# Every fourth unit of weights gets its low part from an accumulating DMA

## The chip, the cores and the metric

The kernel runs on one core of one Trainium2 chip. The metric is the device time of one execution in microseconds. The kernel before takes 2758.89 us, the median of 2 runs (2758.85 to 2758.94).

A core has a matrix engine (TensorE, PE in the profile), a vector engine (VectorE, DVE), a scalar engine (ScalarE, ACT), GpSimd (POOL) and a sync engine (SyncE, SP), each with its own queue of instructions, worked off in order. Transfers are issued from a queue (here almost all from SyncE's) and carried out by 16 DMA engines.

## The reference

A decoder trunk of two layers for 256 tokens of width 2048, all in float32: first a retention layer, then a layer of block-sparse attention; each is followed by a squared-ReLU MLP and a gated embedding of the layer. Cut to its products with weights:

```
h = x
h = h + retention(rms_norm(h, ret_norm_g), ret_w_in, ret_w_out)      # w_in 2048 x 12288, w_out 4096 x 2048
h = h + square(relu(rms_norm(h, mlp_norm_g[0]) @ mlp_w_up[0])) @ mlp_w_down[0]   # 2048 x 8192, 8192 x 2048
h = h + (p[0] @ ple_w_up[0]) * sigmoid(rms_norm(h, ple_norm_g[0]) @ ple_w_gate[0])
k, v = split(rms_norm(h, kv_norm_g) @ w_kv)                          # 2048 x 4096
h = h + attention(rms_norm(h, att_norm_g) @ att_w_q, k, v, rel_bias) @ att_w_o
h = h + mlp(h, layer 1);  h = h + gated embedding(h, layer 1)
return rms_norm(h, final_norm_g)
```

With 256 tokens nearly all of the work is these products, and each weight is read from HBM once.

## The kernel before

**Units.** All weights are cut on the host into units of 128 x 1024 numbers (`UC = 1024`), 968 in all, in the order in which they are used: retention's inputs 0 to 191, its output 192 to 255, the up and down projections of the first MLP 256 to 511, embedding and gate to 547, attention to 675, the second MLP 676 to 931, and embedding and gate to 967. Two units make one transfer of 1024 KB into a tile `raw` of three buffers, issued by SyncE in `load`.

**High and low.** A product in float32 is made of three faster ones in a type of fewer bits (`F32R`): with w = wh + wl and x = xh + xl it is wh xh + wl xh + wh xl. So every unit is converted in `conv`: ScalarE copies `raw` to `wh`, which rounds it (L221), and VectorE subtracts, wl = raw - wh (L222). Both lines are in the helper `split`, which activations use as well. `wh` and `wl` have a ring of `LOOK + 1` = 4 buffers each.

**The loop.** `run` goes over the units in order. For unit i it puts the load of unit i + 6 on SyncE's queue, the conversion of unit i + `LOOK` (3) on ScalarE's and VectorE's, the matmuls of unit i on TensorE's, and then the tasks that were entered for i: emptying PSUM, normalisation, transposes, parts of the attention. There is no scheduler; the order of this code is the order on each queue. Since the ring has four buffers, the conversion of unit i + 3 waits for the matmuls of unit i - 1.

**The matmuls of a unit.** In the up projection and for queries and keys (`phase_a`, `mm_a`, lines L153 and L155) weights are the stationary operand: 8 matmuls of 512 columns with wh and 8 of 256 with wl. Two units make one output tile; the first of them takes high before low, the second (`turned`) low before high. Elsewhere (`phase_b`, `mm_b`, lines L195 to L197) the activations are stationary: 12 matmuls of 512 columns, in threes of which the second reads wl. Products collect in four PSUM banks; `fold` (L226, L227) or the evacuation of the phase empties them.

**The end.** The last project (`last`) keeps its last four units, `hold = LOOK + 1`, until all are there, and then works them off for one half of the tokens and the other, so that the first half's final norm runs beside the second half's matmuls.

Of the kernel before, what the change touches and what calls it, by code (L numbers as in the profile page):

```python
# [10 lines left out]
F32 = mybir.dt.float32  # L11
F32R = mybir.dt.float32r
I32 = mybir.dt.int32
AF = mybir.ActivationFunctionType
ALU = mybir.AluOpType
# [5 lines left out]
KD = D // P  # L21
# [10 lines left out]
NEG = -1e30  # L32
UC = 1024
LEAD = 4
LOOK = 3
WARM = 9
FILL = 5
BR = 32
# [32 lines left out]
class Core:  # L71
# [24 lines left out]
    def conv(self, i):  # L96
        if i >= len(self.units):
            return
        raw = self.raws.pop(i)[:, self.units[i][1] % 2, :]
        wh = self.wp.tile([P, UC], F32R, name=f"wh{i}", tag="wh", bufs=LOOK + 1)  # L100
        wl = self.wp.tile([P, UC], F32R, name=f"wl{i}", tag="wl", bufs=LOOK + 1)
        self.split(wh, wl, raw)
        self.ready[i] = (wh, wl)

    def run(self):
        for fn in self.tasks.pop(-1, []):
            fn()
        for i in range(2, LOOK):
            self.conv(i)
        for i in range(len(self.units)):  # L110
            self.load(i + 6)
            self.conv(i + LOOK)
            wh, wl = self.ready.pop(i)
            self.units[i][2](wh, wl)
            for fn in self.tasks.pop(i, []):
                fn()
        while self.tasks:
            for fn in self.tasks.pop(min(self.tasks)):
                fn()
# [25 lines left out]
    def mm_a(self, ps, wh, wl, rhs, first, last, turned=False):  # L145

        mm = self.nc.tensor.matmul
        cut = [slice(k * P, (k + 1) * P) for k in range(8)]
        for low in (True, False) if turned else (False, True):
            for k, c in enumerate(cut):  # L150
                end = last and k == 7 and low != turned
                if low:
                    mm(ps[:, S:], wl[:, c], rhs[k][:, :S], start=False, stop=end)  # L153
                else:
                    mm(ps, wh[:, c], rhs[k], start=first and k == 0, stop=end)  # L155
# [35 lines left out]
    def mm_b(self, ps, wh, wl, x, t, j, first, last):  # L191

        mm = self.nc.tensor.matmul
        c, a, b = slice(j * 512, (j + 1) * 512), slice(t * P, (t + 1) * P), slice(S + t * P, S + (t + 1) * P)
        mm(ps, x[:, a], wh[:, c], start=first, stop=False)  # L195
        mm(ps, x[:, a], wl[:, c], start=False, stop=False)  # L196
        mm(ps, x[:, b], wh[:, c], start=False, stop=last)  # L197
# [101 lines left out]
    def start(self):  # L299
# [35 lines left out]
        self.xx = {}  # L335
        wh = self.wp.tile([P, UC], F32R, name="wh0", tag="wh", bufs=LOOK + 1)
        wl = self.wp.tile([P, UC], F32R, name="wl0", tag="wl", bufs=LOOK + 1)
        for n in range(2):
# [259 lines left out]
    def last(self, st, src):  # L598


        nc = self.nc
        per, hold = KD // 2, LOOK + 1
        b = len(self.units)
        fin = {"ssq": {}}

        def gains():
            for c in range(4):
                fin["g", c] = self.slot(f"gf{c}")
                row = self.io["gfin"]
                nc.sync.dma_start(fin["g", c], bass.AP(tensor=row.tensor, offset=row.offset + c * 512, ap=[[0, P], [1, 512]]))  # L610
        self.at(b, gains)

        def flip():
            for c in range(4):
                nc.vector.tensor_scalar_mul(fin["g", c], fin["g", c], -1.0 / 8192.0)
        self.at(b + 4, flip)

        def gate(c, t, bank, cuts=1):
            s = self.slot("gt")
            h = self.h[c][:, t]  # L620
            parts = [slice(i * 512 // cuts, (i + 1) * 512 // cuts) for i in range(cuts)]
            if c == 0:
                fin["ssq"][t] = self.cp.tile([P, 4 + t], F32, name=f"fssq{t}")
            for p in parts:
                nc.scalar.activation(s[:, p], bank[:, p], AF.Sigmoid, scale=fin["rn"][:, t:t + 1])
            if cuts > 1:
                scale(0, 1)
            for i, p in enumerate(parts):
                nc.vector.tensor_mul(s[:, p], s[:, p], st["up"][c, t][:, p])
                nc.vector.tensor_add(h[:, p], h[:, p], s[:, p])  # L630
                nc.scalar.activation(self.slot("sq")[:, p], h[:, p], AF.Square, accum_out=fin["ssq"][t][:, c + i:c + i + 1])
            if cuts == 1:
                nc.vector.tensor_mul(h, h, fin["g", c])

        def evac(c, banks, i):
            if c == 0:
                fin["rn"] = self.rn
            for t in range(2):
                gate(c, t, banks[t])
        for c in range(3):  # L640
            self.phase_b(f"gl{c}_", src, c * per, per, lambda k: st["x"][k], lambda banks, c=c: evac(c, banks, 0))
        banks, held = [], []

        def mm(wh, wl, u):
            if u == 0:
                banks.extend(self.bank(f"gl3_{t}_") for t in range(2))
            held.append((u, wh, wl))
            if per - hold <= u < per - 1:
                return
            for t in range(2):  # L650
                for v, h, l in held:
                    for j in range(2):
                        self.mm_b(banks[t], h, l, st["x"][2 * v + j], t, j, v + j == 0, v == per - 1 and j == 1)
                if u == per - 1:
                    if t:
                        gate(3, 1, banks[1], 2)
                        for c in (0, 2, 3):
                            scale(0, c)
                        norm(1)
                        for c in (0, 1, 3, 2):  # L660
                            scale(1, c)
                    else:
                        gate(3, 0, banks[0])
                        norm(0)
            held.clear()

        def norm(t):
            m = self.cp.tile([P, 1], F32, name=f"fm{t}")
            nc.vector.reduce_sum(m, fin["ssq"][t], axis=AX.X)
            fin["r", t] = self.rsqrt(None, m, RMS_EPS, 1, 1.0 / D)  # L670

        def scale(t, c):
            r = fin["r", t]
            h = self.h[c][:, t]
            if (t, c) == (1, 3):
                nc.vector.scalar_tensor_tensor(h, h, r, fin["g", c], op0=ALU.mult, op1=ALU.mult)
            elif c == 0:
                nc.vector.tensor_scalar_mul(h, h, r)
            else:
                nc.scalar.activation(h, h, AF.Copy, scale=r)  # L680
            q = nc.scalar if (t, c) == (1, 2) else nc.sync
            q.dma_start(self.io["out"][t * P:(t + 1) * P, c * 512:(c + 1) * 512], h)
        for u in range(per):
            self.unit(src, 3 * per + u, lambda wh, wl, u=u: mm(wh, wl, u))
# [216 lines left out]
```

## Time and profile before

| | |
|---|---|
| median of the runs shown | 2758.89 us |
| span of the profiled execution, first to last instruction | 2756.9 us |
| TensorE busy | 2743.4 us, 13744 matmuls |
| VectorE busy | 1694.6 us |
| ScalarE busy | 1322.8 us |
| GpSimd busy | 0.2 us |
| conversions of a whole unit, high (L221) | 966, 1051 ns each |
| conversions of a whole unit, low (L222) | 966, 1225 ns each |
| moved by DMA | 522.48 MB, 190 GB/s |

The profiled execution's own time is its span; how it stands to the median is told where the sum is made. A row of a group reads: line, engine, operation, output and inputs with their shapes, count, then busy us and mean ns of one, then the idle time ahead of it and what ended that. A row of the timeline begins with its start and its length in us. A row of waits gives who waited for whom, the sum in us, how often, and the longest. PEld is TensorE's loading of stationary operands, which overlaps with its matmuls.

### The profile page before, as it was taken

To read this page: it belongs to the slowest core of one execution; us is meant where nothing else is said; L and a number is where in the kernel's file an instruction comes from. 1 tells how busy PE (TensorE), PEld (TensorE's weight loads), DVE (VectorE), ACT (ScalarE), POOL (GpSimd) and SP (SyncE) were. 2 spreads that over 40 slices of the span, in tenths; PEclk is the share of its full clock that TensorE was granted. 3 is DMA by queue.
4 is the path that set the end of the run, shared out by engine and by line. 5 is a ranking of instruction groups with operands and counts; after the bars stand their busy time and mean duration, and the time that the engine had idled before them with its cause. 6 is when DMAs were issued, how large, how long until landed. Compare 5 with 4: busy or idle time off the path is not lost.

```text
span 2756.9 us, 34160 instructions
## 1 busy us (share of the span) xinstructions
PE 2743.4 (100%) x13744; PEld 2334.7 (85%) x13744; DVE 1694.6 (61%) x2321; ACT 1322.8 (48%) x1844; POOL 0.2 (0%) x4
## 2 busy tenths in 40 slices
PE   9999999999999999999999999999999999999998
PEld 7888888888888888888888888888888888888886
DVE  6766666655576544665546777775666446664555
ACT  6444444444454433454445555554544334544454
POOL 0000000000000000000000000000000000000000
PEclk9999999999999999999999999999999999999999
DMA  7455555555555555555565555555555555555554
GB/s 277 177 186 186 186 186 186 186 183 186 185 195 186 196 194 190 192 188 192 186 204 188 185 182 179 182 178 185 187 190 192 195 188 196 185 193 189 186 199 153
DMA packets 79450, 522.48 MB, mean 190 GB/s; under 512 B 8987, under 2 KB 12988, under 8 KB 17596
## 3 DMA queue, kind: packets, MB, share of 16 engines
q1 hardware_dynamic: 78476, 519.20, 53.1%
q10 hardware_dynamic: 816, 1.11, 0.3%
q8 instruction: 107, 1.75, 0.3%
q14 instruction: 51, 0.42, 0.0%
HBM read 517.39 MB, written 2.88 MB: 189 GB/s over the span
## 4 chain that ended last, share of the span: by engine, by line
PE 98%; DMA 1%; DVE 0%; ACT 0%; issue 0%; SPq 0%; ACTq 0%; DVEq 0%
PE up L155 17%; PE up L153 9%; PE qk L155 4%; PE aq L155 2%; PE ak L155 2%; PE qk L153 2%; PE aq L153 1%; PE ak L153 1%; PE pu L573 1%; DMA raw<-ret_in 1%; PE xt L255 1%; PE y L461 1%; PE dn__11046 L195 0%; PE dn__20748 L196 0%; PE dn__21353 L197 0%; PE dn__11358 L196 0%
## 5 line engine op out<-in xcount | busy, mean ns | idle before, releaser
L222 DVE TENSOR_TENSOR wl<-raw,wh 128x1024 fp32r<-128x1024 f32 (+1 forms) x971 | 1180.0, 1221 | 652.7 <-ACT wh L221 639.2
L221 ACT CAST wh<-raw 128x1024 fp32r<-128x1024 f32 (+1 forms) x971 | 1013.5, 1048 | 709.3 <-DVE rs_y L278 29.2
L155 PE MATMUL up<-x,wh 128*128 128x512 f32 x2048 | 490.5, 391 | 0.0
L155 PEld LDWEIGHTS up<-x,wh 128*128 128x128 f32 x2048 | 376.1, 188 | 72.4
L153 PEld LDWEIGHTS up<-x,wl 128*128 128x128 f32 x2048 | 263.4, 191 | 10.4
L153 PE MATMUL up<-x,wl 128*128 128x256 f32 x2048 | 266.7, 283 | 0.0
L226 ACT COPY t<-up 128x256 f32<-128x256 f32 x128 | 47.6, 372 | 331.6 <-PE up L155 331.6
L227 DVE TENSOR_TENSOR t<-t,up 128x256 f32<-128x256 f32 x128 | 53.9, 421 | 216.7 <-ACT t L226 216.5
L155 PE MATMUL qk<-x,wh 128*128 128x512 f32 x448 | 109.9, 393 | 0.0
L155 PEld LDWEIGHTS qk<-x,wh 128*128 128x128 f32 x448 | 81.8, 188 | 15.5
L233 ACT ACTIVATE x<-xt,g 128x256 fp32r<-128x256 f32 x112 | 52.5, 478 | 50.6 <-DVE x L234 39.4
L234 DVE SCALAR_TENSOR_TENSOR x<-xt,g,x 128x256 fp32r<-128x256 f32 x112 | 53.0, 481 | 25.7 <-ACT x L233 25.5
L155 PE MATMUL aq<-x,wh 128*128 128x512 f32 x256 | 63.3, 392 | 0.0
L155 PE MATMUL ak<-x,wh 128*128 128x512 f32 x256 | 62.9, 392 | 0.0
L153 PEld LDWEIGHTS qk<-x,wl 128*128 128x128 f32 x448 | 57.4, 191 | 2.2
L153 PE MATMUL qk<-x,wl 128*128 128x256 f32 x448 | 58.1, 283 | 0.0
L533 DVE SCALAR_TENSOR_TENSOR s<-t 128x256 f32<-128x256 f32 x128 | 54.4, 425 | 4.4
L155 PEld LDWEIGHTS ak<-x,wh 128*128 128x128 f32 x256 | 46.7, 189 | 8.7
L155 PEld LDWEIGHTS aq<-x,wh 128*128 128x128 f32 x256 | 46.5, 189 | 8.7
L222 DVE TENSOR_TENSOR a<-s,a 128x256 fp32r<-128x256 f32 x128 | 53.6, 419 | 0.0
L221 ACT CAST a<-s 128x256 fp32r<-128x256 f32 x128 | 52.0, 406 | 0.0
L242 ACT ACTIVATE sq<-h 128x512 f32<-128x512 f32 x48 | 30.1, 628 | 37.5 <-DVE h L542 15.6
(895 smaller groups left out, 4999.3 us busy)
## 6 DMA issues: line engine op xcount, KB each, us to landing
raw<-mlp_up SPq DMA_DIRECT2D x128, 1024.0 KB, 4.8
raw<-mlp_dn SPq DMA_DIRECT2D x128, 1024.0 KB, 4.8
raw<-ret_in SPq DMA_DIRECT2D x94, 1024.0 KB, 4.8
raw<-att SPq DMA_DIRECT2D x48, 1024.0 KB, 4.8
raw<-ret_out SPq DMA_DIRECT2D x32, 1024.0 KB, 4.8
raw<-ple_gate SPq DMA_DIRECT2D x32, 1024.0 KB, 4.8
raw<-att_o SPq DMA_DIRECT2D x16, 1024.0 KB, 4.8
raw<-ple_up SPq DMA_DIRECT2D x4, 1024.0 KB, 4.8
```

The source lines that it names most:

```text
L153: mm(ps[:, S:], wl[:, c], rhs[k][:, :S], start=False, stop=end)
L155: mm(ps, wh[:, c], rhs[k], start=first and k == 0, stop=end)
L221: self.nc.scalar.copy(dst_h, src)
L222: self.nc.vector.tensor_sub(dst_l, src, dst_h.bitcast(F32))
L226: self.nc.scalar.copy(dst, ps[:, :S])
L227: self.nc.vector.tensor_add(dst, dst, ps[:, S:])
L233: self.nc.scalar.activation(t[:, :S], src, AF.Copy, scale=gs)
L234: self.nc.vector.scalar_tensor_tensor(t[:, S:], src, gs, t[:, :S].bitcast(F32), op0=ALU.mult, op1=ALU.subtract)
L242: self.nc.scalar.activation(self.slot("sq"), self.h[c][:, t], AF.Square, accum_out=self.ssq[:, t, c:c + 1])
L255: self.nc.tensor.transpose(ps[:, o * P:(o + 1) * P], self.h[c][:, t, f * P:(f + 1) * P], self.ident)
L461: mm(ys[t], a, w, start=i == 0, stop=i == len(ops) - 1)
L533: nc.vector.scalar_tensor_tensor(s, t, 0.0, t, op0=ALU.max, op1=ALU.mult)
```

## The change

For units from 12 on whose index is 1 modulo 4, VectorE no longer makes the low part. ScalarE copies `raw` to `wh` as before and then writes -wh into `wl`, a copy with scale -1. Then GpSimd issues a DMA that reads the same 512 KB of weights from HBM a second time and adds them to what is in `wl`: raw - wh again. The ring of `wh` and `wl` grows from four to five buffers (`LOOK = 4`), and the conversion of a unit is put on the queues four units ahead rather than three, from the twelfth unit on; up to there it stays at three (`SOON`). The number of units held in the last project is now a constant (`HOLD = 4`), the same as before. The space in SBUF that is kept for the descriptors of software-issued transfers is set to 1024 bytes of a partition.

```diff
-LOOK = 3
+LOOK = 4
+SOON = 3
+HOLD = 4
+EVERY = 4
...
         wh = self.wp.tile([P, UC], F32R, name=f"wh{i}", tag="wh", bufs=LOOK + 1)
         wl = self.wp.tile([P, UC], F32R, name=f"wl{i}", tag="wl", bufs=LOOK + 1)
-        self.split(wh, wl, raw)
+        if i >= 12 and i % EVERY == 1:
+            src, j, _ = self.units[i]
+            self.nc.scalar.copy(wh, raw)
+            self.nc.scalar.activation(wl, wh.bitcast(F32), AF.Copy, scale=-1.0)
+            self.nc.gpsimd.dma_start(wl, self.io[src][j // 2, :, j % 2], accum_op=ALU.add)
+        else:
+            self.split(wh, wl, raw)
         self.ready[i] = (wh, wl)
...
-        for i in range(2, LOOK):
-            self.conv(i)
+        done = 2
         for i in range(len(self.units)):
             self.load(i + 6)
-            self.conv(i + LOOK)
+            while done <= i + (SOON if i < 12 else LOOK):
+                self.conv(done)
+                done += 1
...
-        per, hold = KD // 2, LOOK + 1
+        per, hold = KD // 2, HOLD
...
-    nc = bacc.Bacc("TRN2", target_bir_lowering=False, num_devices=1)
+    nc = bacc.Bacc("TRN2", target_bir_lowering=False, num_devices=1, dynamic_dma_scratch_size=1024)
```

Lines below the edit move by up to ten: L221, L222 and L226 of before are L231, L232 and L236 after; the two new ScalarE lines are L107 and L108, the DMA is L109. How it stands on the queues is shown at two places. The number behind a name is that of the unit or tile and, behind a second underscore, of the buffer; in brackets stand the semaphores that the instruction waits for (DMASW is one of a software-issued transfer, DMAHW one of SyncE's).

On ScalarE's queue, in the second half of the first up projection, before:

```order
L221 CAST wh408_9358<-raw408_9282 128x1024 [waits DMAHW7_49,PE_49,Activation_49]
L226 COPY t_9378<-up1_10_9339 128x256 [waits PE_49]
L221 CAST wh409_9386<-raw408_9282 128x1024 [waits Activation_49]
L221 CAST a10_9383<-s2_9381 128x256 [waits DVE_49]
L221 CAST wh410_9409<-raw410_9333 128x1024 [waits DMAHW0_49,PE_49,Activation_49]
```

The same place after:

```order
L231 CAST wh408_9438<-raw408_9385 128x1024 [waits DMAHW7_49]
L231 CAST a9_9435<-s2_9433 128x256 [waits DVE_49]
L107 CAST wh409_9461<-raw408_9385 128x1024 [waits PE_49]
L108 ACTIVATE wl409_9462<-wh409_9461 128x1024 [waits DMASW6_49,PE_49,Activation_49]
L236 COPY t_9482<-up1_10_9442 128x256 [waits PE_49]
L231 CAST wh410_9490<-raw410_9436 128x1024 [waits DMAHW0_49]
```

Unit 409 is converted one unit earlier, ahead of the copy that empties tile 10, and that copy now stands behind the negation.

On TensorE's queue, where unit 337 begins in the first down projection, before:

```order
L195 MATMUL dn0_1_0__8003<-wh337_7963,a2_6260 128x512 [waits Activation_49]
L196 MATMUL dn0_1_0__8003<-wl337_7964,a2_6260 128x512 [waits DVE_49]
L197 MATMUL dn0_1_0__8003<-wh337_7963,a2_6260 128x512
L195 MATMUL dn0_1_1__8004<-wh337_7963,a2_6260 128x512
L196 MATMUL dn0_1_1__8004<-wl337_7964,a2_6260 128x512
```

The same after:

```order
L205 MATMUL dn0_1_0__8089<-wh337_8030,a2_6328 128x512 [waits Activation_49]
L206 MATMUL dn0_1_0__8089<-wl337_8031,a2_6328 128x512 [waits DMASW1_49]
L207 MATMUL dn0_1_0__8089<-wh337_8030,a2_6328 128x512
L205 MATMUL dn0_1_1__8090<-wh337_8030,a2_6328 128x512
L206 MATMUL dn0_1_1__8090<-wl337_8031,a2_6328 128x512
```

The matmuls are the same and in the same order; the first that reads the low part waits for a transfer in place of VectorE.

## The prediction

> **What bounds the kernel now.** I read the shares of busy time first, then the waits of TensorE, then one stretch of the timeline, and last the transfers.
>
> ```profile
> span 2756.9 us, 34160 instructions
> PE 2743.4 (100%) x13744; PEld 2334.7 (85%) x13744; DVE 1694.6 (61%) x2321; ACT 1322.8 (48%) x1844; POOL 0.2 (0%) x4
> PEclk9999999999999999999999999999999999999999
> PE 98%; DMA 1%; DVE 0%; ACT 0%; issue 0%; SPq 0%; ACTq 0%; DVEq 0%
> PE warm L364 <- DVE zero L357: 1.5, 1, 1.5
> PE qk L182 <- ACT wh L221: 0.8, 2, 0.4
> ```
>
> The first four lines are of the page, the last two are all that the view of waits has for TensorE. A busy TensorE need not be at its peak, since the ends of matmuls are modelled; the waits say it better. In 2756.9 us TensorE waits 1.5 + 0.8 = 2.3 us for another engine, all of it in the first microseconds. The clock is granted nearly in full. So the end is set by the number of matmuls times their spacing, and no other engine has a share in it as long as it delivers on time.
>
> Is the spacing itself stretched by what VectorE, ScalarE or the transfers do beside it? Two windows of 8 us answer that, the first near the end, where the weights have all arrived, the second in a down projection. The columns are PE, PEld, DVE, ACT and POOL busy time with counts, the granted clock, the DMA share and GB/s.
>
> ```profile
> 2737.00:2745.00 8.00, 8.00 (x37) 6.64 (x36) 3.16 (x9) 1.41 (x3) 0.00 (x0) 1.00 0.00 0
> 1001.00:1009.00 8.00, 8.00 (x37) 6.62 (x36) 3.68 (x3) 3.16 (x3) 0.00 (x0) 1.00 0.49 184
> ...
> 2737.15 0.39 PE L196 MATMUL gl__22264<-wl,x 128*128 128x512 f32 x1
> ...
> 2740.33 0.39 PE L195 MATMUL gl__22265<-wh,x 128*128 128x512 f32 x1
> ```
>
> Both hold 37 matmuls, one with no transfer at all and one at 184 GB/s. Between the two starts shown lie 14 spacings: (2740.33 - 2737.15)/14 = 0.227 us. A unit of a projection is 12 such matmuls, 12 x 0.227 = 2.72 us, and that is what the rhythm of the down projection gives too, by its conversions:
>
> ```profile
> 1003.72 1.05 ACT L221 CAST wh<-raw 128x1024 fp32r<-128x1024 f32 x1 [1.67 <-PE dn__8004 L197]
> 1006.44 1.05 ACT L221 CAST wh<-raw 128x1024 fp32r<-128x1024 f32 x1 [1.67 <-PE dn__8004 L197]
> ...
> 1108.01 3.82 PE L155 MATMUL up<-x,wh 128*128 128x512 f32 x16
> 1113.58 3.82 PE L155 MATMUL up<-x,wh 128*128 128x512 f32 x16
> ```
>
> ScalarE converts one unit each 2.72 us and idles 1.67 us before it, for TensorE to give back a buffer. In the up projection two units take 1113.58 - 1108.01 = 5.57 us, 2.78 us each.
>
> **What is removed, and its worth.** Of 968 units, those with index 13, 17, ..., 965 change: 239. Each loses one VectorE subtraction and gains one ScalarE pass.
>
> ```profile
> L222 DVE TENSOR_TENSOR wl<-raw,wh 128x1024 fp32r<-128x1024 f32 x966 | 1177.2, 1225 | 651.1 <-ACT wh L221 637.7 <-PE aq L155 1.0
> L221 ACT CAST wh<-raw 128x1024 fp32r<-128x1024 f32 x966 | 1011.2, 1051 | 707.6 <-DVE rs_y L278 29.2 <-PE dn__18284 L197 26.7 <-PE dn__18008 L197 26.7
> L221 ACT CAST wh<-raw 128x512 fp32r<-128x512 f32 x3 | 1.7, 615 | 0.0
> L680 ACT ACTIVATE h<-h,rs_y 128x512 f32<-128x512 f32 x5 | 3.4, 712 | 1.3 <-DVE rs_y L278 1.3
> ```
>
> VectorE loses 239 x 1.225 = 293 us, from 1694.6 to 1402 us, 51% of the span. Nobody waits for it: TensorE's list of waits has no subtraction in it. So this is worth 0 us.
>
> ScalarE gains 239 scaled copies of 128x1024. A copy without scale costs 1.051 us; at 512 columns a scaled one costs 712 ns against 615, so the bound above is 1.051 + 2 x 0.097 = 1.25 us. I take 1.1: 263 us, from 1322.8 to 1586, 58%. Its cover is the 1.67 us of idle ahead of each conversion; were that gone, the pass would delay the next conversion by 1.1 us, and that has most of four units to spare. What stands behind the pass on ScalarE's queue are the copies that empty PSUM (L226); a bank is asked for again three tiles, some 16 us, later in the up projection. 0 us.
>
> **The wait that is added.** The first matmul on such a low part waited for VectorE and now waits for the transfer, and everything on TensorE's queue stands behind it. So the question of the case is a latency against a window. A unit's buffers come free when the unit five earlier is done, and it is due four units later. The rows of one unit's start, in the down projection (first two) and in the up projection:
>
> ```profile
> 1003.52 0.39 PE L195 MATMUL dn__8003<-wh,a 128*128 128x512 f32 x1
> 1003.74 0.39 PE L196 MATMUL dn__8003<-wl,a 128*128 128x512 f32 x1
> ...
> 1111.66 2.08 PE L153 MATMUL up<-x,wl 128*128 128x256 f32 x16
> ...
> 1111.91 1.05 ACT L221 CAST wh<-raw 128x1024 fp32r<-128x1024 f32 x1
> ```
>
> Down: the cast starts at 1003.72, as shown above, and the low part that it begins is read by the second matmul of the unit four later, 1003.74 + 4 x 2.72 = 1014.62. That is 10.9 us, less the cast, 1.05, the negation, 1.1, and some 0.1 for two hand-overs: 8.7 us are left for GpSimd's issue and the transfer. Up: of the sixteen low matmuls eight end one unit and eight begin the next, so the unit changes at about 1112.7; the cast, which needs only the high buffer, is done at 1112.96, the negation some 1.2 us later, 1114.2, and the low part is due at 1112.7 + 4 x 2.78 = 1123.8: 9.6 us.
>
> What it takes is not in the trace: no row shows GpSimd issuing a transfer, and none an accumulating one. The nearest:
>
> ```profile
> raw<-mlp_up SPq DMA_DIRECT2D x128, 1024.0 KB, 4.8
> h<-xn SPq DMA_DIRECT2D x4, 512.0 KB, 10.6
> out<-h SPq DMA_DIRECT2D x7, 256.0 KB, 2.4
> 17.70 0.56 SPq L370 DMA_DIRECT2D h<-xn  x1
> q1 hardware_dynamic: 78476, 519.20, 53.1%
> ```
>
> Below: a line through 256 KB in 2.4 us and 1024 KB in 4.8 puts a plain 512 KB at 3.2 us, and SyncE's issue at 0.56: 3.8 us. Above: the 512 KB that landed 10.6 us after issue, in the crowded first 30 us, and 1 us for the issue: 11.6. The accumulate moves 512 KB out of HBM and reads as much of its destination, 1024 KB read in all, so I take the row of 1024 KB, 4.8 us, plus 1 us for GpSimd's issue (about twice SyncE's), plus a share of a raw load beside it. That load is due just then, since the pair's raw tile comes free when the cast ends; the load lasts 4.8 us and the DMA is 53% busy, so 1 to 2 us are lost to it: 7.3 us. It fits into 8.7 with 1.4 us to spare, and into 9.6 with 2.3. In bytes the DMA stays below its end too: 239 x 0.5 MB is 125 MB more, or 250 MB where the reading back counts, on 519 MB at 53.1%: 66 to 79%.
>
> The Trainium skill (Collectives: The Full Stack, "The bandwidth ceiling: the fold count and why AG ≠ RS ≠ AR") holds that an add made by the DMA engines costs no time for the adding but two reads for each write, so half the rate of a copy. No run here shows it yet; by that rule the transfer would be about one of 1024 KB, and the sum would stay as it is.
>
> **Edits with one answer.** The ring's fifth buffer and the deeper look-ahead delay nothing: up to unit 12 the conversions keep their distance of three, and in the last project the held units stay at four, so head and tail keep their rows. The smaller descriptor scratch holds far less, but one accumulate is due in 10.9 us; if it made GpSimd wait, that would be part of the latency above. TensorE's instructions stand in the same order.
>
> **Rivals.**
>
> *Late (slower).* If issue and transfer need L instead of 7.3 us and L is over the window, TensorE stalls ahead of such a unit. The next such unit's conversion starts one unit before that stall, so the stall lengthens its window: in the mean each loses half the excess, (L - 8.7)/2 in the projections and (L - 9.6)/2 in the up parts. With the outer 11.6 us: 2.9/2 x 239 = 347 us, or 3106. With 9.6 + 1, a transfer of two raw loads' time: 1.9/2 x 239 = 227, 2986 where every unit were of the narrower kind. It passes 2% (55 us) when L is over 8.7 + 2 x 55/239 = 9.2 us. For it: a kind of transfer without any row, the collision with the raw load, and that an accumulate on engines 53% busy may cost more than its bytes. Against it: even 10.6 us was seen only where all first loads were queued at once. 0.33.
>
> *GpSimd held up by VectorE (slower).* The Trainium skill (SBUF — State Buffer, "Who interferes with whom") says that a VectorE instruction in a two-port mode locks GpSimd out of writing descriptors, and infers that a tensor_tensor does not; by it the chains below would hold nothing up, and no run here shows either. As a mechanism of this kernel, priced as if they did: VectorE is busy beside the negation, in the up projection in chains.
>
> ```profile
> 1110.45 0.42 DVE L227 TENSOR_TENSOR t<-t,up 128x256 f32<-128x256 f32 x1 [1.80 <-ACT t L226]
> 1110.91 0.42 DVE L533 SCALAR_TENSOR_TENSOR s<-t 128x256 f32<-128x256 f32 x1
> 1111.40 1.23 DVE L222 TENSOR_TENSOR wl<-raw,wh 128x1024 fp32r<-128x1024 f32 x1
> 1112.55 0.42 DVE L222 TENSOR_TENSOR a<-s,a 128x256 fp32r<-128x256 f32 x1
> 1112.99 1.22 DVE L222 TENSOR_TENSOR wl<-raw,wh 128x1024 fp32r<-128x1024 f32 x1
> ```
>
> Held for one subtraction, 1.23 us, the latency is 8.5 and still fits. Held for a whole chain, 1114.21 - 1110.45 = 3.8 us, it is 11.1, 1.5 us over the up window and, if every unit met such a chain, 239 x 1.5/2 = 179 us: 2938. But the chain loses its last L222 to this very change, and the projections have single ones. 0.04.
>
> *Faster.* VectorE's subtractions would have to slow the matmuls. The two windows above speak against it: the same 37 matmuls in 8 us with VectorE at 3.16 and 3.68 us, and 0.227 us each in a stretch without it. What TensorE does not fill, 2756.9 - 2743.4 = 13.5 us, is 0.5% and lies in head and tail. 0.01.
>
> *It doesn't do what it says.* The 239 accumulates stand on GpSimd's queue and their units' subtractions are gone from VectorE's, so it does.
>
> **How the numbers follow.** The profiled execution's span of 2756.9 us lies 2.0 below the median of 2758.89; I forecast against the median. Likeliest, 0.62, is that the transfer fits: every term of the sum is 0 on the path, and a microsecond is added for stray stalls where ScalarE is busiest: 2760 us, with a range of its own of 2754 to 2814, the upper end where some hundred of the units are 1 us late and half of that counts. The two slower cases hold 0.37, the faster one 0.01. For 8 in 10 the range must reach into the late case, to about its middle: L of 9.7 us, 1.0/2 x 239 = 119, 2879, taken as 2875. Below, nothing can be won but a part of the 13.5 us in head and tail, which keep their rows: 2754. Two per cent is about what a measurement of this kernel can tell from no change.
>
> **What would show it.** In the changed kernel's trace TensorE's waits should stay near 2.3 us and name no low part; the accumulates should land within some 7 us of issue; VectorE's subtractions should count 727 and VectorE stand at about 51%, ScalarE at 58%. I am wrong if TensorE's waits list a transfer into wl some two hundred times, with longest waits over a microsecond, or if the spacing of 0.227 us itself has changed.

## The result, and the profile after

The changed kernel takes 2790.59 us, the median of 2 runs (2788.81 to 2792.37), against 2758.89: a ratio of 1.0115, with a 95% interval of 1.0086 to 1.0145. It is 31.7 us slower, clear of the noise and under 2%. The profiled execution is the slower of the two, 2792.37 us with a span of 2790.6, so the span to be explained is 2790.6 - 2756.9 = 33.7 us.

The page of the changed kernel, its first rows and the queues:

```profile
PE 2755.8 (99%) x13744; PEld 2336.8 (84%) x13744; DVE 1408.2 (50%) x2082; ACT 1571.3 (56%) x2083; POOL 208.3 (7%) x243
...
q1 hardware_dynamic: 78476, 519.20, 54.6%
q0 software_dynamic: 34416, 125.32, 24.4%
...
L108 ACT ACTIVATE wl<-wh 128x1024 fp32r<-128x1024 f32 x239 | 253.5, 1061 | 7.8 <-ACT wh L107 0.2
...
L109 POOL DMA_DIRECT2D wl<-mlp_dn x64 | 55.7, 870 | 655.1 <-ACT wl L108 583.5
```

VectorE has lost 286 us and ScalarE gained 249, and a transfer costs GpSimd 0.87 us. TensorE is idle for 2790.6 - 2755.8 = 34.8 us in place of 13.5, so 21.3 of the 33.7 us are idle time, and 12.4 are matmuls that took longer. Where the idle time lies, the windows tell (busy time of PE, PEld, DVE, ACT and POOL with counts, then granted clock, DMA share, GB/s). Two stretches of the MLPs:

```profile
800.00:900.00 100.00, 100.00 (x577) 88.42 (x576) 54.05 (x81) 59.37 (x82) 7.82 (x9) 1.00 0.82 236
1000.00:1100.00 100.00, 100.00 (x443) 82.78 (x442) 36.31 (x33) 48.44 (x46) 7.82 (x9) 1.00 0.84 241
```

the same two in the kernel before:

```profile
800.00:900.00 100.00, 100.00 (x577) 88.38 (x576) 65.22 (x91) 50.01 (x72) 0.00 (x0) 1.00 0.54 190
1000.00:1100.00 100.00, 100.00 (x443) 82.86 (x442) 48.66 (x43) 38.95 (x37) 0.00 (x0) 1.00 0.55 198
```

and three in the changed kernel that lost time, near the start and in the last project:

```profile
60.00:80.00 20.00, 17.07 (x71) 13.71 (x70) 10.23 (x16) 9.70 (x13) 1.75 (x2) 0.91 0.67 203
2680.00:2700.00 20.00, 17.38 (x70) 13.93 (x69) 9.84 (x24) 9.50 (x11) 0.86 (x1) 0.91 0.79 255
2720.00:2740.00 20.00, 17.43 (x70) 14.12 (x70) 7.74 (x9) 9.22 (x13) 0.86 (x1) 0.91 0.63 198
```

In the two stretches of the MLPs TensorE is never idle and does as many matmuls in 100 us as before (577 and 443): there nine accumulates in 100 us cost nothing. The loss is local, and in the three windows that lost time the granted clock falls too. The waits name the reason. Here are the three longest, and two others:

```profile
PE g__596 L206 <- DMA wl<-ret_in: 2.9, 1, 2.9
PE gl__22010 L206 <- DMA wl<-ple_gate: 2.6, 1, 2.6
PE gl__22198 L206 <- DMA wl<-ple_gate: 2.6, 1, 2.6
PE aq L163 <- DMA wl<-att: 1.9, 2, 1.0
PE dn__11484 L206 <- DMA wl<-mlp_dn: 1.1, 1, 1.1
```

In all, 21 of the 239 transfers came late (the expectations below count 22 stalls: the other, 0.73 us, is a wait for VectorE), from 0.15 to 2.93 us each, 20.5 us together: nearly all of the new idle time. The last project shows why, and what a stall does afterwards. First ScalarE and GpSimd ahead of the stall of 2.62 us, then TensorE through it:

```profile
2673.24 1.04 ACT L107 CAST wh<-raw 128x1024 fp32r<-128x1024 f32 x1
2674.31 1.06 ACT L108 ACTIVATE wl<-wh 128x1024 fp32r<-128x1024 f32 x1
2674.72 1.96 SPq L620 DMA_DIRECT2D gf<-gfin  x4
2675.78 0.86 POOL L109 DMA_DIRECT2D wl<-ple_gate  x1 [12.15 <-ACT wl L108]
...
2682.68 0.39 PE L205 MATMUL gl__22010<-wh,x 128*128 128x512 f32 x1
2685.69 0.79 PE L206 MATMUL gl__22010<-wl,x 128*128 128x512 f32 x1 [2.62 <-DMA wl<-ple_gate]
2686.28 0.63 PE L207 MATMUL gl__22010<-wh,x 128*128 128x512 f32 x1
2686.71 0.63 PE L205 MATMUL gl__22011<-wh,x 128*128 128x512 f32 x1
...
2690.07 0.39 PE L206 MATMUL gl__22010<-wl,x 128*128 128x512 f32 x1
```

The transfer is issued at 2675.78, beside four loads of the final gains, and lands 9.9 us later, where the median one in the MLPs takes 6.6. After the stall the matmuls come 0.43 us apart, the granted clock is 0.50 from 2686 to 2688, and the 12 spacings to 2690.07 take 4.38 us in place of 12 x 0.227 = 2.72: a stall of 2.6 us costs 1.7 us more behind it, most of it by the clock. That happened behind the three stalls over 2.5 us, 5 us. Most of the other 7 us are restarts: the matmul ahead of a wait runs out its 0.39 us instead of being followed after 0.227, and the first one after it holds its successor for 0.34, some 0.3 us for each of the other 18.

A transfer can be late because it starts late or because it takes long, and the rows tell the two apart. From the end of a regular unit's negation in the down projection 8.9 us are left until TensorE asks for the low part; 0.4 us go into the hand-over to GpSimd, and a transfer of 6.6 us leaves 1.9 to spare. At the stall above 7.7 us were left and the transfer took 9.9, so most of the lateness is the transfer's. At the other stall of the last project, of 2.58 us, it is the negation's. ScalarE's queue was held by the gate's evacuations up to 2711.6, 5.5 us were left, and the transfer took 7.6:

```profile
2708.83 0.67 ACT L635 ACTIVATE gt<-gl__22011,rn 128x512 f32<-128x512 f32 x1
2711.01 0.63 ACT L641 ACTIVATE sq<-h 128x512 f32<-128x512 f32 x1 [1.51 <-DVE h L640]
...
2713.66 1.06 ACT L108 ACTIVATE wl<-wh 128x1024 fp32r<-128x1024 f32 x1
2715.12 0.87 POOL L109 DMA_DIRECT2D wl<-ple_gate  x1 [13.46 <-ACT wl L108]
...
2722.75 0.51 PE L206 MATMUL gl__22198<-wl,x 128*128 128x512 f32 x1 [2.58 <-DMA wl<-ple_gate]
```

Counted in the same way, 4.2 to 8.1 us were left at 13 of the 21 stalls, and the transfers took 5.1 to 9.9. At the other eight 8.7 us or more were left, and the transfers took 8.5 to 10.5.

### The profile page after: what moved, and what is told of

Same layout as the page of the kernel before. It is cut to its first block, busy times and chain, and to the rows that moved or that the text cites. A ratio compares the mean times of both kernels' runs of the same rounds, so it can differ in the third digit from the quotient of the medians.

```text
span 2790.6 us, 34875 instructions
## 1 busy us (share of the span) xinstructions
PE 2755.8 (99%) x13744; PEld 2336.8 (84%) x13744; DVE 1408.2 (50%) x2082; ACT 1571.3 (56%) x2083; POOL 208.3 (7%) x243
## 3 DMA queue, kind: packets, MB, share of 16 engines
q0 software_dynamic: 34416, 125.32, 24.4%
## 4 chain that ended last, share of the span: by engine, by line
PE 87%; DMA 6%; issue 5%; DVE 0%; ACT 0%; POOL 0%; POOLq 0%; SPq 0%
PE up L165 17%; PE up L163 9%; DMA wl<-ret_in 2%; PE qk L165 2%; PE aq L165 2%; DMA wl<-mlp_dn 1%; PE ak L165 1%; PE qk L163 1%; DMA wl<-ple_gate 1%; PE aq L163 1%; PE ak L163 1%; PE y L471 1%; DMA wl<-att 1%; PE xt L265 1%; PE pu L583 0%
## 5 line engine op out<-in xcount | busy, mean ns | idle before, releaser
L232 DVE TENSOR_TENSOR wl<-raw,wh 128x1024 fp32r<-128x1024 f32 (+1 forms) x732 | 888.0, 1220 | 761.9 <-ACT wh L231 753.1
L231 ACT CAST wh<-raw 128x1024 fp32r<-128x1024 f32 (+1 forms) x732 | 761.9, 1046 | 425.4 <-DVE rs_y L288 26.0
L107 ACT CAST wh<-raw 128x1024 fp32r<-128x1024 f32 x239 | 250.8, 1049 | 161.7 <-PE dn__8090 L207 6.7
L108 ACT ACTIVATE wl<-wh 128x1024 fp32r<-128x1024 f32 x239 | 253.5, 1061 | 7.8 <-ACT wh L107 0.2
L236 ACT COPY t<-up 128x256 f32<-128x256 f32 x128 | 47.7, 372 | 270.0 <-PE up L165 270.0
L109 POOL DMA_DIRECT2D wl<-mlp_dn x64 | 55.7, 870 | 655.1 <-ACT wl L108 583.5
L109 POOL DMA_DIRECT2D wl<-mlp_up x64 | 55.6, 870 | 653.0 <-ACT wl L108 619.6
L109 POOL DMA_DIRECT2D wl<-ret_in x45 | 39.3, 873 | 523.6 <-ACT wl L108 380.9
```

The source lines that it names most:

```text
L107: self.nc.scalar.copy(wh, raw)
L108: self.nc.scalar.activation(wl, wh.bitcast(F32), AF.Copy, scale=-1.0)
L109: self.nc.gpsimd.dma_start(wl, self.io[src][j // 2, :, j % 2], accum_op=ALU.add)
L231: self.nc.scalar.copy(dst_h, src)
L232: self.nc.vector.tensor_sub(dst_l, src, dst_h.bitcast(F32))
L236: self.nc.scalar.copy(dst, ps[:, :S])
```

## Experiments

The theory is that time is lost only at the late places, and not by the accumulates as such. Rivals: an even cost of each accumulate, 31.7/239 = 0.13 us; the ring of five or the software queue itself.

### Accumulates in the MLPs alone

```diff
-        if i >= 12 and i % EVERY == 1:
+        if i % EVERY == 1 and (256 <= i < 512 or 676 <= i < 932):
```

> Accumulates only for the units of the two MLPs (128 of the 239); all other units are split on VectorE. Theory (late places): the changed kernel loses time only where a transfer lands after its unit is due; of its 22 such stalls five lie in the MLPs, 1.12 + 0.58 + 0.26 + 0.24 + 0.17 = 2.4 us, with some 0.3 us of slower matmuls behind each: 2762 us. Rival (even cost): each accumulate costs the same, 31.7/239 = 0.13 us, by contention or by a slower start of its unit: 2759 + 128 x 0.13 = 2776 us. Rival (the ring): the fifth buffer, the deeper look-ahead or the mere use of a software queue costs it: 2790 us.

Measured: 2761.22 us (2760.69 to 2764.04) against 2758.72, a ratio of 1.001 [1.0, 1.0019]. TensorE's only wait on a transfer:

```profile
PE dn__11423 L206 <- DMA wl<-mlp_dn: 1.2, 1, 1.2
```

128 of the 239 accumulates cost 2.5 us together, 0.02 us each, and the one stall with its restart accounts for 1.5 of them; the rest is not traced. The even cost falls, and so does the ring. Of the five small stalls that the MLPs had in the changed kernel one is left; why the other four went was not traced.

### The ring alone

```diff
-        if i >= 12 and i % EVERY == 1:
+        if i < 0:
```

> Ring of five and look-ahead of four as in the changed kernel, but no accumulate: every unit is split on VectorE. Late places: 2759 us, as before, with 2.3 us of TensorE waits. Even cost: 2759 us as well. The ring: 2790 us.

Measured: 2759.02 us, a ratio of 1.0 [0.9991, 1.001]. The fifth buffer and the look-ahead are free, as forecast. The smaller scratch has no transfer to serve in this run; in the changed kernel the 239 issues on GpSimd took 0.86 to 1.0 us each, and no wait for the scratch shows.

### The second pass without the transfer

```diff
-            self.nc.gpsimd.dma_start(wl, self.io[src][j // 2, :, j % 2], accum_op=ALU.add)
```

> The changed kernel without the transfers: for every fourth unit ScalarE still writes the negated high part, and nothing is added to it, so these units' low parts are wrong values (-wh in place of w - wh). What is left is ScalarE's second pass and VectorE's relief. Late places, by transfers: TensorE waits for no low part and the time is 2759 to 2760 us. Rival (ScalarE's queue): if the late negations themselves, or the evacuations behind them, hold TensorE, some 10 us of the 32 stay: 2769 us.

Measured: 2759.57 us, a ratio of 1.0003 [0.9994, 1.0012]. VectorE stands at 1406.7 us and ScalarE at 1572.5, as in the changed kernel, and TensorE's waits on either, apart from the 1.5 us at the program's start, are 0.8 and 0.7 us. So 239 subtractions less on VectorE and 239 passes more on ScalarE together move the time by 0.9 us, which the interval cannot tell from nothing. What costs is the transfer.

### A plain copy in place of the accumulate

```diff
-            self.nc.gpsimd.dma_start(wl, self.io[src][j // 2, :, j % 2], accum_op=ALU.add)
+            self.nc.gpsimd.dma_start(wl, self.io[src][j // 2, :, j % 2])
```

> The changed kernel with a plain copy in place of the accumulate, on the same queue behind the same negation; these units' low parts are then w itself and not w - wh. It separates the adding from the moving. By my working an accumulate is priced like 1024 KB: the plain 512 KB should land in 4 to 5 us instead of 6.6, take half of the 24.4% of the DMA engines, and the stalls shrink from 21 us to under 8: 2763 to 2772 us. Rival (the software queue is what is slow): it lands in 6 us or more as well, and the time stays at 2785 to 2790 us.

Measured: 2763.66 us, a ratio of 1.0018 [1.0008, 1.0027]. The queue and the landings (issues, size, median us to landing):

```profile
q0 software_dynamic: 34416, 125.32, 12.9%
...
wl<-mlp_up POOLq DMA_DIRECT2D x64, 512.0 KB, 4.7
wl<-ple_gate POOLq DMA_DIRECT2D x16, 512.0 KB, 5.6
```

and the same rows of the changed kernel:

```profile
wl<-mlp_up POOLq DMA_DIRECT2D x64, 512.0 KB, 6.6
wl<-ple_gate POOLq DMA_DIRECT2D x16, 512.0 KB, 7.3
```

The same 34416 packets and 125.32 MB take the engines 0.129 x 2761.7 = 356 us as copies and 0.244 x 2790.6 = 681 us as accumulates: 1.91 times as much. The adding makes the transfer land 1.9 us later in the up projection and GpSimd's issue longer, 0.87 us against 0.53. With landings 1.9 us earlier two stalls on transfers are left of 21, of 1.1 and 0.9 us. The software queue is not what is slow.

### One buffer more

```diff
-LOOK = 4
+LOOK = 5
```

> The changed kernel with six buffers and a look-ahead of five from unit 12 on. Late places: each window grows by one unit, 2.72 us, and all but one of the stalls were under that, so TensorE's waits fall to 2 to 4 us and the time to 2759 to 2764 us. Even cost: unchanged, 2790 us. The ring: 2790 us or more.

Measured: 2766.41 us (2764.81 to 2768.04), a ratio of 1.0027 [1.0016, 1.0038], a little over the range expected. The window per unit is what decides: with 2.72 us more of it, five stalls on transfers are left, 4.3 us together, three of them in the last project and the longest at 46 us:

```profile
PE v__389 L206 <- DMA wl<-ret_in: 1.5, 1, 1.5
PE gl__22357 L206 <- DMA wl<-ple_gate: 1.4, 1, 1.4
```

Beside them there are two waits of 0.3 us for VectorE, at 14 and at 31 us. Those waits and their restarts account for 6 of the 7.7 us; the rest is not traced.

### The same number at other places

```diff
-        if i >= 12 and i % EVERY == 1:
+        if i >= 12 and i % EVERY == 3:
```

> The changed kernel with index 3 instead of 1 modulo 4: as many accumulates, other places. Late places: in the last project the conversion of units 4 and 5 of eight stands behind the gate on ScalarE's queue and that of 3 and 7 does not, so the stalls of 2.62, 2.58, 1.65 and 1.15 us there go, with the two drops of the clock behind the first two (1.7 us each): about 11 us less; elsewhere stalls move and may come or go: 2770 to 2785 us, with no wait over 1 us in the last project. Even cost or the ring: 2790 us.

Measured: 2782.94 us, a ratio of 1.0088 [1.0072, 1.0103], inside the range, but with the last project misjudged. Its waits were to stay under 1 us and did not:

```profile
PE dn__11168 L206 <- DMA wl<-mlp_dn: 6.3, 1, 6.3
PE gl__22198 L206 <- DMA wl<-ple_gate: 3.0, 1, 3.0
PE gl__22010 L206 <- DMA wl<-ple_gate: 1.3, 1, 1.3
```

I had taken the place on ScalarE's queue for the cause there. Ahead of the stall of 3.0 us the queue shows another one: the gate's evacuation holds back three casts, they then run back to back, and so free raw tiles in one go, whose loads start together and beside the accumulate.

```profile
2704.30 2.94 ACT L231 CAST wh<-raw 128x1024 fp32r<-128x1024 f32 x3
2707.14 1.05 ACT L107 CAST wh<-raw 128x1024 fp32r<-128x1024 f32 x1
2708.22 1.06 ACT L108 ACTIVATE wl<-wh 128x1024 fp32r<-128x1024 f32 x1
...
2707.76 10.63 SPq L96 DMA_DIRECT2D raw<-ple_gate  x4
2709.68 0.87 POOL L109 DMA_DIRECT2D wl<-ple_gate  x1 [11.03 <-ACT wl L108]
...
2720.16 0.50 PE L206 MATMUL gl__22198<-wl,x 128*128 128x512 f32 x1 [2.98 <-DMA wl<-ple_gate]
```

The transfer took 10.4 us where the median one in the MLPs takes 6.6, and 7.9 us were left behind the negation in place of 8.9. So of the lateness 3.8 us are the transfer's and 1.0 the negation's. That the loads beside it made the transfer long is read from the rows; no run moves them away.

The new stall of 6.3 us falls to a unit, 495, whose accumulate is issued while a store of 768 KB of the bias rows is under way, which landed 10.3 us after its issue at 1396.88. From 1400 to 1406 the engines are 0.91 to 0.96 busy and move little, 102 to 144 GB/s; first one of these windows with the columns of those above, then the rows around it:

```profile
1402.00:1404.00 2.00, 2.00 (x11) 1.65 (x10) 0.60 (x1) 1.05 (x1) 0.88 (x1) 1.00 0.91 102
...
1396.88 0.66 ACTq L714 DMA_DIRECT2D bvec<-bv  x1
1402.14 0.88 POOL L109 DMA_DIRECT2D wl<-mlp_dn  x1 [10.99 <-ACT wl L108]
...
1416.96 0.79 PE L206 MATMUL dn__11168<-wl,a 128*128 128x512 f32 x1 [6.30 <-DMA wl<-mlp_dn]
```

The transfer took 14.8 us, although the negation was on time (8.9 us were left). In the changed kernel an accumulate that was issued 1.2 us before this store landed in 6.6 us as usual, and the one of unit 497, issued 0.8 us before the store's end, took 10.5 and stalled TensorE for 1.12. That the store is the cause is read from these rows, since no run leaves it out.

### That unit split on VectorE again

```diff
-        if i >= 12 and i % EVERY == 3:
+        if i >= 12 and i % EVERY == 3 and i != 495:
```

> The kernel with index 3 modulo 4, less the accumulate of unit 495 alone, whose transfer runs beside the store of 768 KB in small packets and stalled TensorE for 6.3 us. Late places: those 6.3 us go, with 1.8 us of the clock's drop behind them and 0.2 of a restart: 2782.9 - 8.3 = 2774.6 us. If the transfers were late for another reason, the stall passes on to the neighbours, units 491 or 499, and less than 3 us are gained: 2780 us or more.

Measured: 2775.53 us (2774.78 to 2778.33), a ratio of 1.0062 [1.0047, 1.0077]: 7.4 us less than with unit 495, where 8.3 were expected. All four runs lie below all four with unit 495. One accumulate of 239 was worth some 7 us, and neither neighbour took its stall over. So a late place can be taken out by itself. The price per stall is less well shown: the two traces differ by 6.0 us of TensorE's idle time and by only 0.5 us of its busy time, because small stalls came and went elsewhere and the drop of the clock only moved. It is gone behind unit 495, and there is one now behind a stall of 2.59 us in the last project, where the run with unit 495 had a stall of 2.98 us and no drop behind it.

### Every second unit

```diff
-EVERY = 4
+EVERY = 2
```

> The changed kernel with every second unit accumulated, 478 in place of 239. The 239 took 24.4% of the 16 DMA engines in 2790.6 us, 681 us, and the raw loads and the rest 55%, 1535 us. Twice as many accumulates ask for 1362 + 1535 = 2897 us of full engines, more than TensorE's 2757: the DMA engines become the bound and the time is 2900 to 3050 us, with hundreds of stalls in the projections too. By bytes read alone, 250 MB more at the loads' price of 2.9 us for 1 MB, it would be 1535 + 725 = 2260 us, still under TensorE, and stalls only double: 2820 us.

Measured: 2913.2 us (2906.18 to 2920.22), a ratio of 1.0559 [1.053, 1.0589]. The engines are full in nearly every slice:

```profile
DMA  9899999999999999999999999999999999999996
q1 hardware_dynamic: 78476, 519.20, 49.1%
q0 software_dynamic: 68832, 250.64, 47.1%
...
wl<-mlp_up POOLq DMA_DIRECT2D x128, 512.0 KB, 8.4
```

The engines' work is the bound: 1535 + 1362 = 2897 us by the rows of the changed kernel, and the time lies 16 us above it. That it comes so close is in part luck. In this run's own rows the accumulates take 0.471 x 2904.4 = 1368 us, as forecast, but the loads only 1426, and the two fill 96% of the span. I had expected hundreds of stalls; the trace has 87 on transfers, some 97 us together, and TensorE's matmuls took 49 us longer. The price by bytes alone, 2820 us, falls.

## Why the prediction was right, and what was off

**What bounds the kernel:** right. TensorE's spacing is its own; the second pass without the transfer relieved VectorE by 288 us and moved the time by 0.9.

**VectorE's relief worth nothing, ScalarE's pass hidden:** right, by the same run. The pass took 1.061 us, near the lower of my two ends.

**The latency against the window:** the sum held for the units it was made for, the MLPs', all but five of 128. I had 1 us for the issue, 4.8 for the transfer and 1.5 for the raw load beside it, 7.3 us from the hand-over on; the trace has 6.6 us from issue to landing, with 0.87 us of GpSimd's issue in it, after a hand-over of 0.4 us where I had allowed 0.1 for both. Taking an accumulate for 1024 KB was right within a tenth: 1.91 copies. That agrees with the rule of the Trainium skill (Collectives: The Full Stack, "The bandwidth ceiling: the fold count and why AG ≠ RS ≠ AR"), that the add costs a second read; the runs here show 1.91 times the engines' time, not which part of the transfer takes it.

**The term that was mis-sized** is "a microsecond is added for stray stalls": it measured 31.7. I had worked the window out for a regular unit and taken the rest of the kernel as like it. The rest is where the negation ends late, behind other work on ScalarE's queue, and as little as 4.2 us were left in place of 8.9, or where other transfers run beside the accumulate, and it took up to 10.5 us (with other places up to 14.8). A row for such a length was there: 10.6 us for 512 KB in a crowded stretch, which I used for a rival in which every unit is late, and not for the few units that are.

**The range** held partly by luck. The sum said 2760 us. The range reached to 2814 for a hundred units 1 us late each, and to 2875 for the late rival; what came was 21 stalls of up to 2.9 us, with restarts and a lower clock behind them, and their sum happens to lie inside.

**The clock** I left out of the prices. Behind each of the changed kernel's three stalls of over 2.5 us came another 1.7 us of slower matmuls.

**Rivals.** The late one decided in kind: TensorE waited for transfers into wl, but for 21 units and not for 239, so its price of 2986 us was far off and the likeliest case's own range, up to 2814, held. The forecast of what the trace would show was half met: VectorE at 50%, ScalarE at 56%, spacing unchanged, median landings of 6.6 us in the MLPs (the longest 10.5), but waits of 23 us rather than 2.3. GpSimd held up by VectorE: the issue took 0.87 us in the down and in the up projection alike, 870 ns on average with VectorE at 36 and at 54% busy, and no issue of the 239 was longer than 1005 ns, so nothing of it shows. Faster: no run was.

None of the kernels run beats the kernel before. With TensorE waiting for 2.3 us in all, moving work off VectorE has nothing to win here.

## To carry to other kernels

Price a transfer that takes an engine's place by latency against window at the worst unit, not at the regular one: list what else is queued on the issuing chain and on the DMA engines at each boundary of stages, since a hidden cost shows first there. An accumulating DMA occupies the engines like a copy of nearly twice its size, so its share has to be added to the loads' before it is called free; and an engine with time to spare, like VectorE here, is not worth relieving.

## What the runs showed that I had not expected

Each of the changed kernel's three stalls over 2.5 us was followed by a granted clock that fell to 0.50 in a window of 2 us (0.91 over the 20 us window), while its stalls of 1.75 us and below left it at 1.00. Length alone doesn't decide it: behind the stall of 2.98 us of the run at other places the granted clock was 1.00 in every window of 2 us, and in the run without unit 495 a stall of 2.59 us at the same place brought it down to 0.50.

Beside a store of 768 KB the engines were over 0.9 busy at 102 to 144 GB/s for 6 us, and an accumulate issued in that time landed after 14.8 us in place of 6.6.

An accumulate costs GpSimd 0.87 us to issue, a plain copy of the same shape 0.53.
